# Hybrid attention and HGRN2 block on one core: q and k stored by other rows, loaded in one transfer and earlier; scores ahead of transposes; the merge's sums in another order

## The chip, the core and the metric

The kernel runs on one core of a Trainium2 chip, as one program. TensorE (PE) multiplies, VectorE (DVE), ScalarE (ACT) and GpSimd (POOL) do the elementwise work, SyncE (SP) and GpSimd issue DMA transfers, which 16 DMA engines carry. The metric is the time of the program on the device in microseconds; less is better.

## The reference

One encoder layer on x of 1024 tokens x 1024 channels, all in float32. From `h = rms_norm(x)` one input projection makes everything else:

```python
z = jnp.einsum('bsd,dc->bsc', h, w_in[layer].astype(f32))
qkv_a, g_a, q_b, zf_fwd, zf_bwd, i_b, g_b, zgate_a, zgate_b = jnp.split(z, split_points, axis=-1)
```

Branch A is dilated window attention: three groups of 8 heads of 64 channels, dilation 1, 4 and 16, 64 keys to each side. q and k are normed per head; scores get a bias by relative distance, then a softmax. The three groups' outputs are merged per head by their softmax denominators and multiplied by `silu(g_a)`. Branch B is a gated linear recurrence, forward and backward, over 8 heads of 128 channels. Each branch is projected to 1024 channels:

```python
merged = jax.nn.sigmoid(zgate_a) * y_a + jax.nn.sigmoid(zgate_b) * y_b
h_res = h_res + jnp.einsum('bsd,de->bse', merged, w_out[layer].astype(f32))
```

## The kernel before, in words

**Products.** A float32 product is made of three float32r products: each operand is split into a high part and a low part (hi x hi, hi x lo, lo x hi). Weights come in pages of 128 x 512 from DRAM; ScalarE makes the high part `whi` (a copy), and VectorE, GpSimd or an accumulating DMA the low part `wlo` (the page less `whi`); `Builder.low` names which. A ring of nine split pages stands between that work and TensorE.

**Stages.** In order of time: the norm of x and the values of attention (to 142 us in the profile); the *block stage*, in which most of the input projection is done in 27 blocks, each of which forms a 2 x 2 block product with seven products instead of eight (`run_quads`, to about 668 us); *attention*, mixed with further wide products (to about 845); the *merge* of the three groups, under wide products too (to about 933); the recurrence of branch B (to about 1220); and the two output projections, again by seven products.

**The order of the work.** The program is written by a planner, while it is built. `Plan` keeps a modelled time for each engine. Tasks wait in a list with a priority and are emitted by `tick` as soon as their inputs are ready by the model, lowest priority number first; small products of TensorE (scores, transposes, values) wait in another list, and `burst` emits those that are ready between wide products, in the order of their kind. Each engine then runs its own list strictly in that order, and semaphores hold an instruction until what it needs is there. So an instruction that waits holds all that stands behind it on its engine.

**The block stage.** SP loads the raw pages as pairs, `qraw`, into a ring of three. For each of the seven products of a block ScalarE splits a page; VectorE forms differences of pages for four of them. Results of the q and k blocks are normed (squares on ScalarE, sums by a product `nss`, a Newton step on VectorE), and `scaled` writes them, in the order of residues modulo the dilation, into a ring of four tiles `ny`; its task `out` stores a tile of 128 x 512 to `qkD` in DRAM, in pieces of 2 KB, 512 or 128 bytes per row by the dilation. There are 48 such stores, 16 for each group; half of those of group 2 are in pieces of 2 KB. A tile of `ny` is written again only when its store is done with it.

**Attention.** `attention_start` ends the block stage's pools, opens those of attention, and adds its loads: four pages of h that were set aside (`back_load`), then for each group and half of the heads k, q, the bias, and eight tiles of values. `load_heads` brings a megabyte of q or k in four transfers of 32 partitions each, since the rows of a head pair lie in `qkD` by channel. `scores` (kind 3) writes to PSUM `sc`; VectorE adds the bias and finds the maximum, ScalarE takes the exponentials; `turn` and `turn_pairs` (kind 1) transpose them (`pT`); `pv` (kind 2) multiplies by the values (`o`). Small products of 64 x 64 or 64 x 128 tiles share TensorE's array; the transposes use it whole.

**Merge.** `spread_al` spreads the weights of the three groups by a product (`al`), and six operations of VectorE multiply, sum and gate.

Of the kernel before, what the change touches and what calls it, by code (L numbers as in the profile page):

```python
# [9 lines left out]
F32R = mybir.dt.float32r  # L10
# [3 lines left out]
OP = mybir.AluOpType  # L14
# [4 lines left out]
S = 1024  # L19
# [15 lines left out]
VR, PT = 10, 8  # L35
# [200 lines left out]
class Builder:  # L236
# [56 lines left out]
    def burst(self, merge, most=None):  # L293

        k = 0
        for t in sorted(self.small, key=lambda t: (t.kind, t.seq)):
            if t not in self.small or (t.prio and not merge):
                continue
            if max(self.when(t) + self.SLACK, self.bank.when(t.banks)) > self.p.t["pe"]:
                continue  # L300
            if self.bank.room(t.banks) and (t.room is None or t.room()):
                self.small.remove(t)
                t.fn()
                k += 1
                if most is not None and k >= most:
                    break
        return k
# [348 lines left out]
def hybrid_block(ctx, tc, a, out):  # L656
# [641 lines left out]

    att = {}

    def attention_start(now=False):
        if att or not (now or (not b.small and b.quiet())):
            return
        b.drain()
        gctx.close()
        sctx.close()
        p = hctx.enter_context(tc.tile_pool(name="h10b", bufs=1, side="right"))
# [3 lines left out]
        for n, k, shape in (("v", VR, [128, 256]), ("q", 2, [128, 2, S]), ("k", 2, [128, 2, S]),  # L1311
                            ("s", 6, [128, 3, 4, 64]), ("pt", PT, [128, 2, 2, 128]), ("os", 2, [128, 2, 2, 128]),
                            ("bias", 2, [128, 4, 256])):
            att[n] = b.ring(ap, "a" + n, k, shape)
        for e in range(2):
            hq[e][1, 0] = p.tile([128, 4, 512], F32R, name=f"hb{'hl'[e]}")
        for c in range(4):
            b.task("sp", [], lambda c=c: back_load(c), 1, stage.soon)
        for o, g in enumerate((2, 1, 0)):
            for hv in range(2):  # L1320
                soon = lambda n, k=2 * o + hv: att[n].soon() and (k == 0 or b.wire(3.5))
                for n, f in (("k", load_k), ("q", load_q), ("bias", load_bias)):
                    b.task("sp", [], lambda g=g, hv=hv, f=f: f(g, hv), 2, lambda n=n, soon=soon: soon(n))
                for i in range(8):
                    b.task("sp", [], lambda g=g, hv=hv, i=i: load_v(g, hv, i), 2, lambda soon=soon: soon("v"))

    def back_load(c):
        t = stage.get()
        s_.dma_start(t, h10D[c])
        b.task("act", [t], lambda: back_split(c, t), 2)  # L1330

    def back_split(c, back):
        hi, lo = hq[0][1, 0][:, c], hq[1][1, 0][:, c]
        a_.activation(hi, back, AF.Copy)
        v_.tensor_tensor(lo, back, hi.bitcast(F32), op=OP.subtract)
        stage.done(back)
        att["h"] = att.get("h", 0) + 1

    QT, KT, BIAS, V, left = {}, {}, {}, {}, {"in": 0, "out": 0, "turned": 0}

    def load_heads(t, at):
        for j in range(2):
            for col in range(2):
                s_.dma_start(t[64 * j + 32 * col:64 * j + 32 * col + 32],
                             at[col].rearrange("(p j c) t -> j c p t", p=2, j=2)[j])

    def load_k(g, hv):
        KT[g, hv] = att["k"].get()
        load_heads(KT[g, hv], qkD[g, hv, 2:4])
        score_tasks(g, hv)  # L1350

    def load_q(g, hv):
        QT[g, hv] = att["q"].get()
        load_heads(QT[g, hv], qkD[g, hv, 0:2])
        score_tasks(g, hv)

    def load_v(g, hv, i):
# [239 lines left out]
    def merge_maybe(now=False):  # L1597
# [140 lines left out]
    def evac_qe(h, u):  # L1738
# [4 lines left out]
            store(qD[h, u], t)  # L1743
        return f

    for pr in range(2):
        grs = [tok_group(pos, 128 * i, evac_early(pr, i), last=(i >= 6)) for i in range(8)]
        for k in range(7):
            if pr == 0 and k == 4:
                attention_start(True)  # L1750
                b.until(lambda: att.get("h", 0) == 4)
            b.run_unit(grs[k:k + 1] if k < 6 else grs[6:])
            attention_start()
            merge_maybe()
# [835 lines left out]
```

## Time and profile before

| | before |
|---|---|
| time, median of 3 runs (lowest to highest) | 1420.7 us (1419.35 to 1420.76) |
| the profiled execution | 1421.55 us |
| its span, from the first to the last instruction | 1419.8 us |
| mean granted TensorE clock | 0.997 |
| TensorE busy | 1404.7 us (99%) |
| VectorE, ScalarE, GpSimd busy | 932.6, 840.7, 356.6 us |
| moved by DMA | 230.29 MB, mean 162 GB/s |

Times in the profile are microseconds from the start of the span, mean durations of groups are nanoseconds. A matmul's end is modelled and overlaps the next one's start, so what counts of TensorE is the distance between starts: 0.23 us for a wide product of 512 columns. A row of the waits reads: who, who ended the wait, total us, times, longest. A row of the DMA issues reads: what is written and from what, the issuing queue, how often, KB each, and the median us from issue to landing, where the trace has all its marks. The chain of waits is followed back from the last instruction: start, length, what.

### The profile page before, as it was taken

Reading aid. Unit: us, or ns where it says so; the run is one execution under the profiler, and the core shown is the slowest. Engines: PE = TensorE matmul, PEld = TensorE weight load, DVE = VectorE, ACT = ScalarE, POOL = GpSimd, SP = SyncE. Lnnn points to the kernel's source line nnn. Section 1 sums busy time; section 2 is a strip of 40 time slices with the busy share of each in tenths; the row PEclk is TensorE's granted clock in tenths of the full one; section 3 lists DMA queues with packets and bytes.
Section 4 is the critical chain, followed back from the end, with each engine's and each line's share of the span. In section 5 each row is a group of like instructions: output and inputs, shape, how many; then the busy total and the mean of one; then the engine's idle time right before and its main releaser. Section 6 shows DMA issues by size and latency. Waiting matters only on the chain.

```text
span 1419.8 us, 23915 instructions
## 1 busy us (share of the span) xinstructions
PE 1404.7 (99%) x8506; PEld 1168.3 (82%) x8506; DVE 932.6 (66%) x1889; ACT 840.7 (59%) x1831; POOL 356.6 (25%) x379
## 2 busy tenths in 40 slices
PE   9999999999999999999899999999999999999998
PEld 8788888788888888888778888888888888888887
DVE  6673556776776776331356657887878786358973
ACT  7743554665655646444577553577778784558461
POOL 0101434545433443334032110122222221001011
PEclk9999999999999999999999999999999999999999
DMA  7846568667633344423999429554444452778665
GB/s 238 187 134 188 171 183 190 146 174 172 165 102 99 96 123 136 157 104 126 251 264 261 134 67 318 177 141 124 114 120 120 116 137 73 233 243 218 185 166 137
DMA packets 178915, 230.29 MB, mean 162 GB/s; under 512 B 42227, under 2 KB 102923, under 8 KB 178284
## 3 DMA queue, kind: packets, MB, share of 16 engines
q1 hardware_dynamic: 160988, 193.19, 44.8%
q0 software_dynamic: 16944, 35.40, 13.8%
q8 instruction: 67, 1.10, 0.3%
q14 instruction: 52, 0.43, 0.1%
q10 hardware_dynamic: 864, 0.19, 0.1%
HBM read 168.77 MB, written 81.43 MB: 176 GB/s over the span
## 4 chain that ended last, share of the span: by engine, by line
PE 82%; DVE 7%; DMA 4%; ACT 4%; issue 2%; SPq 0%; POOL 0%; DVEq 0%; ACTq 0%; POOLq 0%
PE gp L60 26%; PE qA L60 18%; PE qE L60 9%; PE sA L60 6%; PE sE L60 5%; PE qC L60 4%; PE u L60 3%; PE oB L60 3%; PE sc L60 2%; PE o L60 2%; DMA qraw<-in_w_in_dram 2%; PE pT L60 1%; DVE ny L60 1%; PE U L60 1%; DMA raw<-in_w_in_dram 1%
## 5 line engine op out<-in xcount | busy, mean ns | idle before, releaser
L60 POOL TENSOR_TENSOR wlo<-qraw,whi 128x512 fp32r<-128x512 f32 x135 | 187.6, 1396 | 375.0 <-ACT whi L60 374.5
L60 ACT ACTIVATE whi<-qraw 128x512 fp32r<-128x512 f32 x189 | 117.8, 626 | 113.8 <-DVE qraw L60 53.1
L60 PE MATMUL gp<-hh,whi 128*128 128x512 f32 x264 | 109.8, 416 | 0.0
L60 DVE TENSOR_TENSOR qraw<-qraw,qraw 128x512 f32<-128x512 f32 x81 | 83.5, 1032 | 34.3 <-DMA qraw<-in_w_in_dram 21.1
L60 PE MATMUL gp<-hh,wlo 128*128 128x512 f32 x264 | 103.8, 393 | 0.0
L60 PE MATMUL gp<-hl,whi 128*128 128x512 f32 x264 | 103.1, 391 | 0.0
L60 ACT ACTIVATE as<-as,neg 128x192 f32<-128x192 f32 (+1 forms) x192 | 77.7, 409 | 25.7 <-DVE neg L60 25.7
L60 PE MATMUL qA<-hh,whi 128*128 128x512 f32 x216 | 84.0, 389 | 0.0
L60 PE MATMUL qA<-hl,whi 128*128 128x512 f32 x216 | 84.0, 389 | 0.0
L60 PE MATMUL qA<-hh,wlo 128*128 128x512 f32 x216 | 84.0, 389 | 0.0
L60 PE MATMUL gp<-whi,hh 128*128 128x512 f32 x192 | 79.6, 414 | 1.0 <-ACT stage L60 1.0
L60 ACT ACTIVATE whi<-raw 128x512 fp32r<-128x512 f32 x92 | 57.3, 626 | 34.4 <-DMA raw<-in_w_in_dram 10.7
L60 POOL COPY mm<-Bc 128x8 f32<-128x8 f32 x64 | 32.6, 539 | 177.7 <-DVE Bc L60 177.7
L60 PE MATMUL gp<-wlo,hh 128*128 128x512 f32 x192 | 75.7, 394 | 0.4 <-DVE wlo L60 0.4
L60 PE MATMUL gp<-whi,hl 128*128 128x512 f32 x192 | 75.5, 393 | 0.0
L60 DVE TENSOR_TENSOR wlo<-qraw,whi 128x512 fp32r<-128x512 f32 x54 | 37.6, 696 | 52.4 <-ACT whi L60 51.4
L60 DVE CUSTOM_DVE_ANT_0 as<-sc,abias 128x192 f32<-128x192 f32 (+1 forms) x192 | 48.6, 308 | 21.6 <-PE sc L60 11.3
L60 POOL DMA_DIRECT2D wlo<-in_w_in_dram x36 | 31.1, 863 | 114.3 <-ACT wlo L60 97.7
L60 PEld LDWEIGHTS gp<-hh,wlo 128*128 128x128 f32 x264 | 49.5, 188 | 11.1
L60 PEld LDWEIGHTS gp<-hh,whi 128*128 128x128 f32 x264 | 49.8, 189 | 8.3
L60 PEld LDWEIGHTS gp<-hl,whi 128*128 128x128 f32 x264 | 49.9, 189 | 8.0
L60 ACT ACTIVATE stage<-gp 128x512 f32<-128x512 f32 x39 | 22.7, 589 | 54.5 <-PE gp L60 43.7
(317 smaller groups left out, 4146.2 us busy)
## 6 DMA issues: line engine op xcount, KB each, us to landing
raw<-in_w_in_dram SPq DMA_DIRECT2D x84, 256.0 KB, 3.6
qraw<-in_w_in_dram SPq DMA_DIRECT2D x60, 256.0 KB, 3.6
qraw<-in_w_in_dram SPq DMA_DIRECT2D x24, 512.0 KB, 4.3
qkD<-ny SPq DMA_DIRECT2D x48, 256.0 KB, 3.3
wlo<-in_w_in_dram POOLq DMA_DIRECT2D x36, 256.0 KB, 4.3
sg<-sgD SPq DMA_DIRECT2D x32, 256.0 KB, 2.9
eraw<-wsD SPq DMA_DIRECT2D x32, 256.0 KB, 3.0
sgD<-stage SPq DMA_DIRECT2D x26, 256.0 KB, 2.2
```

Source lines behind the costliest of these rows:

```text
L60: got = f(*args, **kw)
```

## The change

It does six things.

1. *Stores.* The rows of q and k get another order in `qkD`: the row of a channel is now at 64 i + 32 x + c instead of in its own block of 128, so that a store of 128 rows goes to four places of 32 consecutive rows each.
2. *Loads.* With that order q or k of four heads is one transfer of 128 partitions instead of four of 32 (`load_heads` is gone).
3. *Room.* The pools for q, k and transposed weights, and the place for the four pages of h, move to the right side and are opened by a new `attention_room`, called right behind the block stage; the loads of h and of the first k and q become tasks there, with priority 1.5, and `quiet` does not count them.
4. *Burst.* While `eager` (in attention) the transposes, kind 1, are sorted as 3.5, behind values (2) and scores (3).
5. *Low parts.* From the merge on, `low` is "pool" instead of "dve": GpSimd makes the low parts of the pages there.
6. *Sums.* `spread_al` writes the second product in place in PSUM and adds all to `near`; there are still six operations.

```diff
-        for t in sorted(self.small, key=lambda t: (t.kind, t.seq)):
+        for t in sorted(self.small, key=lambda t: (t.kind if t.kind != 1 or not self.eager else 3.5, t.seq)):
...
-        return all(t.fn in (self.split_next_page, self.feed) for t in self.tasks)
+        return all(t.prio == 1.5 or t.fn in (self.split_next_page, self.feed) for t in self.tasks)
...
-            to = qkD[g, hv, 2 * e + col]
+            to = qkD[g, hv].rearrange("a p t -> (a p) t")[256 * e:256 * e + 256].rearrange("(i x c) t -> i x c t", i=4, x=2)[:, col]
             if g == 2 and e == 1:
-                s_.dma_start(to[:, 512 * half:512 * half + 512], o)
+                s_.dma_start(to[:, :, 512 * half:512 * half + 512], o)
             else:
-                s_.dma_start(to.rearrange("p (r u) -> p r u", r=R)[:, :, n * half:n * half + n],
+                s_.dma_start(to.rearrange("i p (r u) -> i p r u", r=R)[:, :, :, n * half:n * half + n],
                              o.rearrange("p (r u) -> p r u", r=R))
...
+    def attention_room():
+        sctx.close()
+        p = hctx.enter_context(tc.tile_pool(name="h10b", bufs=1, side="right"))
+        ap = actx.enter_context(tc.tile_pool(name="attnR", bufs=1, side="right"))
+        for n, k, shape in (("q", 2, [128, 2, S]), ("k", 2, [128, 2, S]), ("pt", PT, [128, 2, 2, 128])):
+            early[n] = b.ring(ap, "a" + n, k, shape)
+        for e in range(2):
+            hq[e][1, 0] = p.tile([128, 4, 512], F32R, name=f"hb{'hl'[e]}")
+        for c in range(4):
+            b.task("sp", [], lambda c=c: back_load(c), 1.5, stage.soon)
+        for f in (load_k, load_q):
+            b.task("sp", [], lambda f=f: f(2, 0), 1.5)
...
-    def load_heads(t, at):
-        for j in range(2):
-            for col in range(2):
-                s_.dma_start(t[64 * j + 32 * col:64 * j + 32 * col + 32],
-                             at[col].rearrange("(p j c) t -> j c p t", p=2, j=2)[j])
...
-        KT[g, hv] = att["k"].get()
-        load_heads(KT[g, hv], qkD[g, hv, 2:4])
+        KT[g, hv] = early["k"].get()
+        s_.dma_start(KT[g, hv], qkD[g, hv, 2:4].rearrange("a p t -> p a t"))
...
-        b.low = "dve"
+        b.low = "pool"
...
-        v_.tensor_tensor(nat(acc, 1), nat(al[1], 1), per(1), op=OP.mult)
+        v_.tensor_tensor(nat(al[1], 1), nat(al[1], 1), per(1), op=OP.mult)
         v_.tensor_tensor(nat(far, 2), nat(al[2], 2), per(2), op=OP.mult)
+        v_.tensor_tensor(near, near, al[1], op=OP.add)
         v_.tensor_tensor(near, near, far, op=OP.add)
-        v_.tensor_tensor(acc, acc, near, op=OP.add)
-        v_.tensor_tensor(acc, acc, gate, op=OP.mult)
+        v_.tensor_tensor(acc, near, gate, op=OP.mult)
...
+    attention_room()
     for pr in range(2):
```

Three places show how the instructions move. First SP's queue in the last third of the block stage: stores of a q and k block from `ny` tiles to `qkD`, and the loads of the next block's pages behind them. The last numbers of a row are the counts of the transfer's destination, outermost first. Before, and then with the change:

```order
L60 DMA sgD<-stage_4386 128x512
L60 DMA sgD<-spare_4511 128x512
L60 DMA qkD<-ny_4497 128x512
L60 DMA qkD<-ny_4495 128x512
L60 DMA qkD<-ny_4571 2048x1x32
L60 DMA qraw_4636<-in_w_in_dram 128x512 x2
```

```order
L60 DMA sgD<-stage_4386 128x512
L60 DMA sgD<-spare_4511 128x512
L60 DMA qkD<-ny_4497 4x32x512
L60 DMA qkD<-ny_4495 4x32x512
L60 DMA qkD<-ny_4571 4x512x32
L60 DMA qraw_4636<-in_w_in_dram 128x512 x2
```

No row has moved here; the destinations have 4 as their outermost count, where 128 and 2048 stood. The same holds for all 48 stores, and up to the last product of the block stage TensorE's rows are the same.

Second SP's queue at the start of attention: `gaD` is the last store of the block stage, `stage<-h10D` the four pages of h, `ak` and `aq` k and q, `abias` the bias.

```order
L60 DMA gaD<-spare_5854 128x512
L60 DMA raw_5874<-in_w_in_dram 128x2x256
L60 DMA ibD<-stage_5888 128x512
L60 DMA stage_5905<-h10D 128x512
L60 DMA stage_5907<-h10D 128x512
L60 DMA ak_5909<-qkD 32x2x1024 x4
L60 DMA aq_5914<-qkD 32x2x1024 x4
L60 DMA abias_5919<-skewD 64x4x64 x2
```

```order
L60 DMA gaD<-spare_5854 128x512
L60 DMA stage_5877<-h10D 128x512
L60 DMA stage_5879<-h10D 128x512
L60 DMA stage_5881<-h10D 128x512
L60 DMA ak_5883<-qkD 128x2x1024
L60 DMA aq_5885<-qkD 128x2x1024
L60 DMA raw_5893<-in_w_in_dram 128x2x256
L60 DMA ibD<-stage_5911 128x512
L60 DMA stage_5924<-h10D 128x512
L60 DMA abias_5926<-skewD 64x4x64 x2
```

k and q are one row each and stand ahead of the next weight page and of the store of `ibD`, which needs a product behind the block stage; the bias stays behind them.

Third TensorE in attention, behind the second scores of group 2: `sc` are scores, `pT` transposes, `gp` wide products.

```order
L60 MATMUL sc_6193<-ak_5909,aq_5914 64x64
L60 MATMUL sc_6192<-ak_5909,aq_5914 64x64
L60 MATMUL gp_6162<-whi_5708,hbh 128x512
L60 MATMUL gp_6162<-wlo_5709,hbh 128x512
L60 MATMUL gp_6162<-whi_5708,hbl 128x512
L60 MATMUL pT_6233<-ident,as_6026 128x128 x2
L60 MATMUL pT_6233<-ident,as_6027 128x128 x2
L60 MATMUL gp_6162<-whi_5731,hbh 128x512
```

```order
L60 MATMUL sc_6192<-ak_5883,aq_5885 64x64
L60 MATMUL sc_6193<-ak_5883,aq_5885 64x64
L60 MATMUL pT_6220<-ident,as_6039 128x128 x2
L60 MATMUL pT_6220<-ident,as_6040 128x128 x2
L60 MATMUL gp_6139<-whi_5752,hbh 128x512
L60 MATMUL gp_6139<-wlo_5753,hbh 128x512
```

Transposes now follow the scores in one burst instead of standing between wide products.

More of the change, by code (lines that the diff above doesn't have):

```diff
@@ L1299, in hybrid_block @@
     att = {}
+    early = {}
+    def attention_room():
[10 more added lines that the diff above has]
+            b.task("sp", [], lambda f=f: f(2, 0), 1.5)
     def attention_start(now=False):
@@ L1305, in attention_start @@
         gctx.close()
-        sctx.close()
-        p = hctx.enter_context(tc.tile_pool(name="h10b", bufs=1, side="right"))
         psum(2)
@@ L1310, in attention_start @@
         ap = actx.enter_context(tc.tile_pool(name="attn", bufs=1))
-        for n, k, shape in (("v", VR, [128, 256]), ("q", 2, [128, 2, S]), ("k", 2, [128, 2, S]),
-                            ("s", 6, [128, 3, 4, 64]), ("pt", PT, [128, 2, 2, 128]), ("os", 2, [128, 2, 2, 128]),
+        att.update(early)
+        for n, k, shape in (("v", VR, [128, 256]), ("s", 6, [128, 3, 4, 64]), ("os", 2, [128, 2, 2, 128]),
                             ("bias", 2, [128, 4, 256])):
             att[n] = b.ring(ap, "a" + n, k, shape)
[L1315 to L1318, printed above, removed]
         for o, g in enumerate((2, 1, 0)):
@@ L1321, in attention_start @@
                 soon = lambda n, k=2 * o + hv: att[n].soon() and (k == 0 or b.wire(3.5))
-                for n, f in (("k", load_k), ("q", load_q), ("bias", load_bias)):
+                for n, f in (("k", load_k), ("q", load_q), ("bias", load_bias))[2 if o == hv == 0 else 0:]:
                     b.task("sp", [], lambda g=g, hv=hv, f=f: f(g, hv), 2, lambda n=n, soon=soon: soon(n))
@@ L1329, in back_load @@
         s_.dma_start(t, h10D[c])
-        b.task("act", [t], lambda: back_split(c, t), 2)
+        b.task("act", [t], lambda: back_split(c, t), 1.5)
     def back_split(c, back):
@@ L1336, in back_split @@
         stage.done(back)
-        att["h"] = att.get("h", 0) + 1
+        blk["h"] = blk.get("h", 0) + 1
     QT, KT, BIAS, V, left = {}, {}, {}, {}, {"in": 0, "out": 0, "turned": 0}
-    def load_heads(t, at):
-        for j in range(2):
-            for col in range(2):
-                s_.dma_start(t[64 * j + 32 * col:64 * j + 32 * col + 32],
-                             at[col].rearrange("(p j c) t -> j c p t", p=2, j=2)[j])
     def load_k(g, hv):
-        KT[g, hv] = att["k"].get()
-        load_heads(KT[g, hv], qkD[g, hv, 2:4])
+        KT[g, hv] = early["k"].get()
+        s_.dma_start(KT[g, hv], qkD[g, hv, 2:4].rearrange("a p t -> p a t"))
         score_tasks(g, hv)
     def load_q(g, hv):
-        QT[g, hv] = att["q"].get()
-        load_heads(QT[g, hv], qkD[g, hv, 0:2])
+        QT[g, hv] = early["q"].get()
+        s_.dma_start(QT[g, hv], qkD[g, hv, 0:2].rearrange("a p t -> p a t"))
         score_tasks(g, hv)
@@ L1750, in hybrid_block @@
                 attention_start(True)
-                b.until(lambda: att.get("h", 0) == 4)
+                b.until(lambda: blk.get("h", 0) == 4)
             b.run_unit(grs[k:k + 1] if k < 6 else grs[6:])
```

## The prediction

> **What bounds the kernel now.** I read the busy shares first, then the chain of waits by stage, then the waits of TensorE alone.
>
> ```profile
> PE 1404.7 (99%) x8506; PEld 1168.3 (82%) x8506; DVE 932.6 (66%) x1889; ACT 840.7 (59%) x1831; POOL 356.6 (25%) x379
> 142.00:300.00 158.00, 156.75 (x691) 129.13 (x690) 101.01 (x121) 93.17 (x164) 70.73 (x62) 1.00 0.66 172
> 300.00:450.00 150.00, 150.00 (x664) 124.20 (x663) 104.32 (x121) 87.10 (x152) 62.36 (x50) 1.00 0.55 145
> 450.00:550.00 100.00, 100.00 (x443) 82.81 (x442) 74.41 (x86) 59.63 (x104) 39.07 (x26) 1.00 0.41 108
> 550.00:660.00 110.00, 110.00 (x487) 91.09 (x486) 44.86 (x54) 49.57 (x84) 38.26 (x30) 1.00 0.38 126
> ```
>
> The first line is the page's, the others are the table by stretches (start:end, length, then busy us of TensorE, its weight loads, VectorE, ScalarE, GpSimd, granted clock, DMA share, GB/s). TensorE has no idle time to speak of: whatever is removed elsewhere is worth nothing unless TensorE waited for it, and whatever makes TensorE wait is paid in full. From 142 to 668 us run the 27 blocks of seven products (the block stage); it stands at 516.75 busy of 518. But the chain of waits in that stage is not TensorE's everywhere:
>
> ```profile
> 205.99 2.73 PE qA L60 x12
> ...
> 218.07 7.69 DMA qraw<-in_w_in_dram
> ...
> 231.47 4.97 DMA qkD<-ny
> ...
> 239.60 7.66 DMA qraw<-in_w_in_dram
> ...
> 260.78 6.44 DMA qraw<-in_w_in_dram
> ```
>
> For 85 us (208 to 293) it goes through loads of weights and one of the very stores that the change rewrites: there a transfer that lands later moves the end. Elsewhere in the stage it is TensorE alone. Its waits, in the block stage (first line) and from 655 to 860:
>
> ```profile
> PE qA L60 <- ACT spare L60: 0.8, 1, 0.8
> ```
>
> ```profile
> PE sc L60 <- DMA aq<-qkD: 3.8, 2, 2.2
> PE gp L60 <- ACT stage L60: 2.2, 2, 1.2
> PE o L60 <- issue: 0.5, 1, 0.5
> ```
>
> So two places can move: the start of attention, where there is something to gain, and the block stage, where there is something to lose.
>
> **The stores of q and k, 48 of 256 KB.** TensorE's program is the same to the last product of the block stage; there only the destinations of these stores differ, and their outermost count falls from 128, 512 or 2048 to 4. I ask how many of the 16 DMA engines then carry one. What the traces show of shape:
>
> ```profile
> q1 hardware_dynamic: 160988, 193.19, 44.8%
> ...
> qraw<-in_w_in_dram SPq DMA_DIRECT2D x60, 256.0 KB, 3.6
> ...
> qkD<-ny SPq DMA_DIRECT2D x48, 256.0 KB, 3.3
> ...
> sgD<-stage SPq DMA_DIRECT2D x26, 256.0 KB, 2.2
> ak<-qkD SPq DMA_DIRECT2D x24, 256.0 KB, 6.2
> aq<-qkD SPq DMA_DIRECT2D x24, 256.0 KB, 8.8
> ...
> og<-oD SPq DMA_DIRECT2D x12, 512.0 KB, 5.2
> ...
> oh<-in_c_onehot_dram SPq DMA_DIRECT2D x1, 148.5 KB
> ...
> tabD<-tbs SPq DMA_DIRECT2D x3, 12.0 KB
> ```
>
> No transfer of before has 4 outside, so the price is bounded. Below: it is spread as now, and costs nothing. Above: one engine for each outermost row, four in all. I take the upper end, because the nearest rows are narrow ones: loads of 256 KB into 32 partitions (ak, aq) take 6.2 and 8.8 us where 128 partitions take 3.6, and twice the bytes (og) only 5.2. The Trainium skill, "DMA: Bandwidth & Descriptors", section "Why a DMA increments its semaphore by 16 and not by 1", says that a transfer runs on the largest number of engines up to 16 that divides the outermost dimension of both sides; for 4 and 128 that is four. The trace does not contradict it: the transfers with 33 and 8 rows (oh, tabD) are among the few without a landing time in this table, which a completion counted otherwise would explain; by the page the sum below stands as it is, and by an even spread it would be 32 us less.
>
> The price: queue q1 kept 0.448 x 16 x 1419.8 = 10,180 engine-us busy for 193.19 MB, 19.0 KB per engine-us. A store of 262,144 bytes is 13.8 engine-us: 0.86 us on each of 16, 3.45 on each of four. Stores in small pieces cost more. The landings of qkD alone, in 308:452 (512-byte pieces) and in 455:482 (128-byte pieces, one landing), beside those of sgD in 140:660 (2 KB, minimum 2.0):
>
> ```profile
> DMA to landing us min/median/max: 2.6/2.6/4.3
> ```
>
> ```profile
> DMA to landing us min/median/max: 4.2/4.2/4.2
> ```
>
> ```profile
> DMA to landing us min/median/max: 2.0/2.2/4.6
> ```
>
> Of the differences 0.2 us is a longer issue (its own durations go from 319 to 603 ns). That leaves 0.4 and 2.0 us more per engine: 1.26 and 2.9 on 16, 5.0 and 11.4 on four; for the 128-byte pieces, one landing under load, I take 8, between 5.0 and 11.4. With 24, 16 and 8 stores of the three kinds the four engines get 83 + 80 + 64 = 227 us instead of about 57: 170 us more in 526, on a share of 0.52, so 0.85. They can carry it, but what queues behind a pair of stores comes late. Two places on SP's queue:
>
> ```profile
> 215.04 2.94 SPq L60 DMA_DIRECT2D qkD<-ny  x2
> 218.07 2.00 SPq L60 DMA_DIRECT2D qraw<-in_w_in_dram  x2
> ```
>
> ```profile
> 455.22 1.59 SPq L60 DMA_DIRECT2D qkD<-ny  x2
> 456.90 3.37 SPq L60 DMA_DIRECT2D qraw<-in_w_in_dram  x3
> ```
>
> A load uses all engines and is done when the last four are. Behind the pair of 215 us it is late by 2 x 3.45 less the 3.0 us since the first store, about 4; behind 512-byte pairs by 2 x 5.0 - 3 = 7; behind the pair of 455 us by 2 x 8 - 2 = 14. In SP's order such a pair stands right ahead of a block's first load 4, 3 and 3 times for the three kinds; the other pairs have time to drain. ScalarE and VectorE split the pages in program order, so a late page also holds the PSUM copies behind it, and TensorE waits for those. How much it can take: the load of 239.60 came after 7.66 us instead of 3.6, 4 late, and TensorE idled 0.8, so the reserve was 3 us there; between 208 and 293, where two of the four late loads of the first kind and the quoted store lie on the chain itself, there is none; and from 300 us on, with DMA shares of 0.55 and less, I give it 6. Sum: 3 x 4 + 2 x (4 - 3) = 14 for the first kind, 3 x (7 - 6) = 3, 3 x (14 - 6) = 24: 41 us; with the 128-byte pieces at 5.0 it is 14 + 3 + 3 x (8 - 6) = 23. I take the middle, **+32 us**. Bounds: 0 if spread; with a reserve of 3 everywhere 14 + 12 + 33 = 59, and three long waits that each bring the clock loss of the next paragraph, 3 x 3.4, so 69.
>
> **The start of attention.** The change loads q, k and the four pages of h ahead of the first bias and values, q and k in one transfer each instead of four narrow ones. At the old place TensorE waited 3.8 us for aq (quoted), and then ran slow:
>
> ```profile
> 685.00:700.00 15.00, 11.21 (x128) 9.19 (x128) 6.50 (x57) 6.74 (x33) 0.56 (x1) 0.77 1.01 258
> ```
>
> A clock of 0.77 over 15 us is 3.4 us of full clock lost; the part of it that fell in the wait costs nothing, 2.5 fell into work. The Trainium skill, "TensorE: Matmul & The Clock Gate", Part 1, has the clock halve after an idle window of about 3.4 us; the two waits here, 3.8 us together, agree with it.
>
> In SP's new order k, q and three pages of h stand right behind the block stage, ahead of the first ib store; the scores come 78 products of 0.23 us behind its last product (72 before), 18 us. At the 258 GB/s of this stretch the 2 MB and 0.75 MB take 11 us. So the wait goes, and the slow clock with it: gain 3.8 + 2.5 = **6.3**; if the bias, which now stands last, is late instead, half of it.
>
> **The burst's order.** What a change of kind costs TensorE (scores sc, wide products gp, transposes pT):
>
> ```profile
> 767.19 1.57 PE L60 MATMUL sc<-ak,aq 64*128 64x192 f32 x16
> 768.69 0.50 PE L60 MATMUL gp<-whi,hh 128*128 128x512 f32 x1
> 769.03 0.39 PE L60 MATMUL gp<-wlo,hh 128*128 128x512 f32 x1
> ...
> 769.49 0.60 PE L60 MATMUL pT<-ident,as 128*128 128x128 f32 x4
> 769.85 0.48 PE L60 MATMUL gp<-whi,hh 128*128 128x512 f32 x1
> 770.17 0.39 PE L60 MATMUL gp<-wlo,hh 128*128 128x512 f32 x1
> ```
>
> Starts 0.23 us apart are the plain pace. After scores the first product takes 0.34: 0.11 for leaving the small tiles. Around transposes (0.36 + 0.32 against 4 x 0.11 + 0.23) it is 0.01: free. By the two orders scores or values are followed by a wide product 33 times before and 11 now; 21 times now a transpose follows them, which never happened before. Its price lies between 0, if only wide products pay, and the same 0.11: the gain is between 22 x 0.11 = 2.4 and 0.1. I take half, **1.2**. The other waits of attention (2.2 + 0.5) hang on ScalarE's queue and stay.
>
> **Merge.** Sixteen low parts move from VectorE to GpSimd:
>
> ```profile
> 860.00:935.00 75.00, 75.00 (x341) 62.10 (x340) 65.06 (x106) 40.09 (x71) 9.49 (x17) 1.00 0.77 251
> ```
>
> ```profile
> L60 POOL TENSOR_TENSOR wlo<-qraw,whi 128x512 fp32r<-128x512 f32 x135 | 187.6, 1396 | 375.0 <-ACT whi L60 374.5
> L60 DVE TENSOR_TENSOR wlo<-qraw,whi 128x512 fp32r<-128x512 f32 x54 | 37.6, 696 | 52.4 <-ACT whi L60 51.4
> ```
>
> GpSimd gets 16 x 1.4 = 22 us in 75 where it works 9.5, VectorE loses 11; the six operations of the merge stay six. TensorE is busy 75.00 of 75: nothing. If GpSimd were late with a page, 0.7 us each, 11 at most.
>
> **Sum.** The profiled execution took 1421.55 us (span 1419.8, 1.75 around it): + 32 - 6.3 - 1.2 = 1446.1. Its run lies 0.85 above the median of 1420.7, so I predict **1445**.
>
> **Rivals.** *The stores are spread as before* (chance 0.21): then only the gains remain, 1420.7 - 7.5 = 1413, and 1410 if attention's other waits (2.7) go too. For it: the bytes, pieces and 128 source partitions are the same. Against it: the narrow rows above. It decides from the number of engines: at 16 nothing is late. *Four engines, but the pages' ring of nine swallows most of it* (0.05): nine pages are 9 x 2.72 = 24 us of products, so a loss of 5 to 10 is possible if the ring is full; with the gains, 1418 to 1423. Against it: the 0.8 us idle at a load only 4 us late. *Attention loses* (0.04): with transposes last, values come later, VectorE's and ScalarE's copies bunch, and waits like the quoted 1.2 us appear five times more; with even stores 1420.7 - 6.3 + 12 = 1426. Only under the first rival would this decide the sign, from a loss of 7.5.
>
> The forecast itself has 0.70, with a range of its own of 1428 to 1470. The whole range of 8 in 10 reaches into the first rival: 1411 to 1470. A measurement of this kernel tells 0.2%, 2.8 us, from no change; faster 0.21, same 0.05, slower 0.74.
>
> **What will show it.** Right: the block stage is longer by some 32 us, mostly past 450 us, with waits of qA, qE, qC for ScalarE and of whi for qraw; the row of qkD<-ny has no landing time or a longer one; DMA share there hardly changes; attention starts without the wait for aq. Wrong: a block stage of 526 us; or a wait of sc for abias in place of aq; or more time between the first scores and the last values than before.

## The result, and the profile after

The changed kernel takes **1491.2 us** (median; 1489.67 to 1491.8), the kernel before 1420.0 beside it: a ratio of 1.0501, 95% interval 1.0485 to 1.0517. The forecast was 1445, range 1411 to 1470: the sign is right, the size is not. The loss is 71 us and not 25.

The page's head and its row of the stores, after:

```profile
span 1489.2 us, 23884 instructions
PE 1427.4 (96%) x8506; PEld 1179.1 (79%) x8506; DVE 928.6 (62%) x1873; ACT 839.6 (56%) x1831; POOL 381.0 (26%) x395
q1 hardware_dynamic: 159836, 193.18, 42.0%
qkD<-ny SPq DMA_DIRECT2D x48, 256.0 KB
```

TensorE, at 99% before, is at 96%. The engines' total work on queue q1 has not grown: 0.420 x 1489.2 = 625 us of all 16, 636 before. The stores' row has lost its landing time, and so have the rows of all other transfers on SP's queue, so the landings are read from single marks further below.

Where the time went is read from the block stage's ends. The chain of waits at its first product and at the first product behind it, before:

```profile
142.52 2.72 PE qA L60 x12
...
669.34 1.16 PE gp L60 x6
```

and after:

```profile
142.30 2.72 PE qA L60 x12
...
739.82 17.68 PE gp L60 x78
```

526.8 us before, 597.5 after: 70.7 more, of 69.4 more in the whole span. All else together gave back 1.3. What the 70.7 are, the waits of TensorE in that stretch and the table by stretches show (qA is one of a block's products, nss the norm's sums, `stage` and `spare` copies out of PSUM; columns as in the prediction; the table has the whole stage before in one row, then after in five stretches and as a whole):

```profile
PE qA L60 <- DVE stage L60: 12.6, 2, 7.0
PE qA L60 <- ACT stage L60: 12.1, 5, 4.5
PE qA L60 <- ACT spare L60: 10.8, 5, 4.7
PE nss L60 <- ACT nhi L60: 6.7, 2, 3.4
PE nss L60 <- DVE ny L60: 2.5, 1, 2.5
PE nss L60 <- DVE nlo L60: 2.2, 3, 0.9
```

```profile
142.52:669.34 526.82, 525.58 (x2318) 434.53 (x2317) 326.15 (x382) 292.74 (x509) 214.81 (x170) 1.00 0.52 143
```

```profile
142.30:300.00 157.70, 147.44 (x627) 119.71 (x627) 89.01 (x106) 79.10 (x141) 62.09 (x53) 0.97 0.60 155
300.00:400.00 100.00, 86.86 (x356) 70.08 (x355) 60.87 (x67) 46.00 (x81) 41.63 (x37) 0.93 0.59 138
400.00:500.00 100.00, 90.97 (x384) 73.52 (x383) 60.54 (x73) 54.41 (x96) 31.99 (x24) 0.97 0.36 105
500.00:600.00 100.00, 89.61 (x374) 72.45 (x373) 60.22 (x67) 45.26 (x79) 32.46 (x21) 0.95 0.38 85
600.00:739.80 139.80, 135.54 (x583) 110.99 (x582) 55.80 (x71) 66.51 (x113) 49.96 (x37) 0.98 0.42 128
142.30:739.80 597.50, 550.42 (x2317) 446.74 (x2317) 326.43 (x382) 291.28 (x509) 218.14 (x170) 0.96 0.48 126
```

The waits sum to 46.9 us, against 1.2 before. By the first and the last row of the table TensorE's idle time grew from 526.82 - 525.58 = 1.2 to 597.50 - 550.42 = 47.1 us, and its busy time grew by 24.8 us for the same products: together (45.8 and 24.8 before rounding) they are the 70.7. The granted clock of the stage is 0.96 where it was 1.00. The trace has ten periods in it at a clock of 0.50, 47.8 us together, so 23.9 us of full clock; for 7.2 of the 47.8 us TensorE was idle anyway, which leaves 20.3 that fell into work. So about a third of the loss is not waiting but the slow clock behind the waits. And the loss lies in every stretch: TensorE's idle time is 10.3, 13.1, 9.0, 10.4 and 4.3 us in the five stretches.

Two ways lead from a store to TensorE. The waits of ScalarE in the same stretch, before and after:

```profile
ACT whi L60 <- DVE qraw L60: 48.9, 29, 4.1
...
ACT ny L60 <- DMA qkD<-ny: 3.0, 3, 2.4
```

```profile
ACT whi L60 <- DVE qraw L60: 122.3, 48, 9.9
ACT ny L60 <- DMA qkD<-ny: 34.3, 12, 5.6
```

The first row is the pages that come late, which the prediction had. Part of that lateness is already in the issue: on SP's queue the longest issue of a page's load took 2.4 us before and 5.9 after, that of a store 0.6 and 5.2; why is not shown. The second row is a tile of `ny` that can't be written again until its store has landed, which it had not. Both stand on the chain of waits of after, in the region 217 to 262 us:

```profile
221.70 10.36 DMA qraw<-in_w_in_dram
...
237.74 10.73 DMA qkD<-ny
...
251.60 7.71 DMA qraw<-in_w_in_dram
```

### The profile page after: what moved, and what is told of

It reads as the page before. It is cut to its first block, busy times and chain, and to the rows that moved or that the text cites. A ratio compares the mean times of both kernels' runs of the same rounds, so it can differ in the third digit from the quotient of the medians.

```text
span 1489.2 us, 23884 instructions
## 1 busy us (share of the span) xinstructions
PE 1427.4 (96%) x8506; PEld 1179.1 (79%) x8506; DVE 928.6 (62%) x1873; ACT 839.6 (56%) x1831; POOL 381.0 (26%) x395
## 4 chain that ended last, share of the span: by engine, by line
PE 65%; DMA 12%; DVE 11%; ACT 7%; issue 3%; SPq 1%; POOL 0%; DVEq 0%; ACTq 0%; POOLq 0%
PE gp L60 26%; PE qA L60 8%; PE sA L60 6%; DMA qraw<-in_w_in_dram 6%; DMA qkD<-ny 6%; PE sE L60 4%; DVE ny L60 4%; PE qE L60 3%; PE u L60 3%; PE oB L60 3%; PE sc L60 2%; DVE qraw L60 2%; PE qC L60 2%; PE pT L60 2%; PE o L60 2%
## 5 line engine op out<-in xcount | busy, mean ns | idle before, releaser
L60 POOL TENSOR_TENSOR wlo<-qraw,whi 128x512 fp32r<-128x512 f32 x135 | 191.3, 1427 | 442.4 <-ACT whi L60 427.5
L60 DVE TENSOR_TENSOR qraw<-qraw,qraw 128x512 f32<-128x512 f32 x81 | 79.4, 981 | 87.3 <-DMA qraw<-in_w_in_dram 77.4
L60 PE MATMUL qA<-hh,whi 128*128 128x512 f32 x216 | 87.1, 403 | 12.8 <-DVE stage L60 12.6
L60 PE MATMUL qA<-S2h,whi 128*128 128x512 f32 x108 | 47.5, 440 | 22.9 <-ACT stage L60 12.1
L60 POOL COPY mm<-Bc 128x8 f32<-128x8 f32 x64 | 32.6, 539 | 129.0 <-DVE Bc L60 124.5
L60 PEld LDWEIGHTS qA<-hh,whi 128*128 128x128 f32 x216 | 42.3, 196 | 23.6 <-DVE stage L60 13.9
L60 POOL TENSOR_TENSOR wlo<-raw,whi 128x512 fp32r<-128x512 f32 x33 | 43.0, 1310 | 59.9 <-ACT whi L60 55.6
```

The source lines that it names most:

```text
L60: got = f(*args, **kw)
```

## Experiments: is it the four places, and how does the price grow?

**Sixteen places and eight.** One number of the store's destination. The two expectations say that the channels get mixed; that was an error of mine: with 8 or 16 places a channel stays inside its head, and q and k are exchanged alike, so the same is computed.

```diff
-  .rearrange("(i x c) t -> i x c t", i=4, x=2)[:, col]
+  .rearrange("(i x c) t -> i x c t", i=16, x=2)[:, col]
```

(`i=8` in rows8.)

> The changed kernel with one number of the stores other: 128 rows go to sixteen places of 8 rows instead of four of 32. The pieces, the bytes, the number of transfers and the order on every engine are the same; the rows then lie in another order than the loads of attention read, so that q and k come with their channels mixed and the output is another, which costs no time. Theory (the four outermost places put a store on four DMA engines, and all of the loss is in the block stage): sixteen marks for each store, block stage about 527 us as before, and in all 1491 less 70, about 1420; if the gain of 7.5 us forecast for attention was there and only hidden by the disturbance, 1413. Rival (it is the split destination itself, its more scattered rows or its descriptor of one more dimension, that costs): still near 1490.

> As the run with sixteen places, but eight of 16 rows (the output is another for the same reason). Theory: eight marks for each store and half the lateness of each; if the loss follows the lateness in proportion, about 1455; if waits shorter than a reserve of about 3 us are swallowed, as the prediction had it, 1420 to 1435. Rival of the scattered rows: about 1490.

Measured: sixteen places 1421.0 us, ratio to before 0.9997 (0.9985 to 1.0008); eight places 1435.1, ratio 1.0098 (1.0072 to 1.0125). The block stage of the two:

```profile
142.86:670.80 527.94, 526.34 (x2318) 434.25 (x2317) 328.39 (x382) 292.05 (x509) 216.85 (x170) 1.00 0.54 142
```

```profile
142.30:685.70 543.40, 530.99 (x2318) 436.24 (x2317) 328.87 (x382) 291.82 (x509) 215.25 (x170) 0.99 0.52 138
```

The pieces, the number of transfers and the order of the engines are those of the changed kernel, so neither the scattered rows nor the descriptor's form costs anything: the number of engines does. The semaphore marks of single stores in the trace (us from the issue to each mark) say it directly:

```
 4 places, 492.91 us:  0.94 | 5.43 5.68 6.74 6.87
 8 places, 214.92 us:  1.05 | 3.93 4.01 4.13 4.28 4.45 4.59 4.60 5.02
16 places, 215.38 us:  3.21 3.23 3.31 3.41 3.62 3.65 3.66 3.72 3.75 3.76 3.77 3.80 3.81 3.83 3.84 3.94
```

Four, eight and sixteen landings, and with less than sixteen one early mark beside them. This is what the Trainium skill states in "DMA: Bandwidth & Descriptors", section "Why a DMA increments its semaphore by 16 and not by 1" (the largest number up to 16 that divides the outermost dimension of both sides; each of these engines counts its own landing, and the issuing queue writes the rest at once); the trace agrees, with 4, 8 and 16 landings and the one early mark. By these marks the last landing of the 48 stores comes after a median of 3.4 us before, 3.8 with sixteen places, 5.1 with eight and 8.0 with four. The price grows faster than that: 0, 14 and 70 us.

**Half of the stores spread, and the groups one by one.**

```diff
+            if hv == 1:
+                for i in range(4):
+                    d, s = to[i], o[32 * i:32 * i + 32]
...
+                        s_.dma_start(d.rearrange("p (r u) -> p r u", r=R)[:, :, n * half:n * half + n],
+                                     s.rearrange("p (r u) -> p r u", r=R))
```

and, for one group at a time (`g == 2` in narrow_g2):

```diff
-  .rearrange("(i x c) t -> i x c t", i=4, x=2)[:, col]
+  .rearrange("(i x c) t -> i x c t", i=4 if g == 1 else 16, x=2)[:, col]
```

> The changed kernel with the stores of one half of the heads (24 of 48) written as four transfers of 32 rows each, the same rows at the same places, so that each of them is spread again; the other 24 go to four places at once as before. Theory: each narrow store costs by itself, so half of the 70 us is left, about 1455. Rival (the four engines are merely overloaded, and it is the backlog from one pair to the next that costs): well over half goes, 1430 or less.

> The changed kernel with four places for the sixteen stores of group 1 (pieces of 512 bytes) alone, and sixteen places for the other 32 stores. The prediction's sum gave these sixteen stores 3 us (three pairs, each 7 late against a reserve of 6). Rival, after the runs with eight places and with half of the stores narrow: every narrow store costs about the same, 70 / 48 = 1.5 us, so about 23 us here, 1440 to 1448.

> Four places for the sixteen stores of group 2 alone (eight in pieces of 128 bytes, eight of 2 KB), sixteen places for the others. The prediction's sum has 24 us for the pieces of 128 bytes and a third of 14 for the others: 29, about 1450. By the run with group 1 alone (23.6 us for sixteen stores) every narrow store costs about 1.5 us whatever its pieces: 1445. If the three groups' losses add, group 0 would be left with 70 less both.

Measured: half spread 1465.4 us (ratio 1.0314, 1.0286 to 1.0341); group 1 alone 1444.6 (1.0167, 1.0135 to 1.0199); group 2 alone 1442.9 (1.0152, 1.0125 to 1.0178). Over the run with sixteen places group 1 costs 23.6 us and group 2 21.9, some 1.4 to 1.5 us for a narrow store in both, whatever its pieces (two executions each, so some 4 us to either side of the 23.6 and the 21.9). 70.2 less both leaves 24.7 for group 0, the same again, if the groups add; group 0 alone was not run. The sum of the prediction, 3 us for group 1 and 29 for group 2, does not hold: group 1 by far, group 2 by 7 us. Half spread lost 44, not 35; it also writes the other 24 stores in 96 transfers of 64 KB, and what those cost by themselves was not measured, so it settles nothing beside the others.

**Two parts.** 64 rows of each store to four places, 64 to sixteen:

```diff
+  for h, i in ((0, 4), (1, 16)):
+      to = rows[256 * e + 128 * h:256 * e + 128 * h + 128].rearrange("(i x c) t -> i x c t", i=i, x=2)[:, col]
+      part = o[64 * h:64 * h + 64]
```

> The changed kernel with each store in two transfers of 64 rows: one to four places of 16 rows, the other to sixteen places of 4. The channels stay inside their heads, so the output is the same. By the price of the prediction (13.8 engine-us for 256 KB) the four busiest engines then have 1.73 + 0.43 = 2.2 us for a store, against 3.45 with four places and 1.73 with eight. Theory (what counts is how long the busiest engine has with a store): a little over the run with eight places (1435), so 1436 to 1448. Rival (what counts is that a transfer is narrow at all): as with four places, 1480 to 1490.

Measured: 1439.5 us (ratio 1.0128, 1.0101 to 1.0154). So four engines are not a fault in themselves. Ordered by the time that the busiest engine has with a store, by the prediction's price of 13.8 engine-us: 0.86, 1.73, 2.2 and 3.45 us, the loss is 0, 14, 18 and 70 us.

## Experiments: by which way does a late store reach TensorE?

**One ring longer.** Room for it comes from `spare`, five tiles instead of seven, which has a run of its own as the control.

```diff
-QRAW, SPARE = 3, 7
+QRAW, SPARE = 3, 5
-        blk["y"] = b.ring(p, "ny", 4, [128, 512])
+        blk["y"] = b.ring(p, "ny", 6, [128, 512])
```

The first pair of lines is spare5, both are spare5_ny6, and spare5_q4 has `4, 5` in the first alone.

> A control for the next two: the changed kernel (four places) with the ring of PSUM copies, spare, at five tiles instead of seven, which frees room. Theory: the ring is not what ends the waits, so 1490 to 1500, some more at most.

> As the control, with the freed room given to the ring of ny, six tiles instead of four: a late store then holds the norm's tiles less. In the changed kernel 35.1 us of idle time ahead of instructions on ny were ended by the landing of a store (3.0 before). If the late ny is what TensorE waits for in the end, a third or more of the 70 us goes: under 1468. If the late pages behind the stores are (the prediction's only path), nothing goes: the control's time within 5 us.

> As the control, with the freed room given to the ring of raw pages, qraw, four pairs instead of three: loads are issued one pair earlier, so a late page is late by less. If late pages are what TensorE waits for, a third or more of the 70 us goes: under 1468. If late ny is, the control's time within 5 us. If both are needed, neither of the two gains much alone.

Measured: control 1494.8 us, six `ny` 1477.8, four pairs of pages 1473.1 (ratios 1.0520, 1.0401 and 1.0367, the intervals some 0.004 to each side for the first two and 0.003 for the third). Neither gains a third of the 74 us, and neither stays within 5 us of the control, so both ways count and neither is the only one. The waits of ScalarE, of the control, of six `ny` and of four pairs:

```profile
ACT whi L60 <- DVE qraw L60: 121.1, 43, 9.3
...
ACT ny L60 <- DMA qkD<-ny: 8.1, 5, 3.3
```

```profile
ACT whi L60 <- DVE qraw L60: 139.6, 52, 9.1
```

```profile
ACT ny L60 <- DMA qkD<-ny: 46.7, 17, 6.5
...
ACT whi L60 <- DVE qraw L60: 24.2, 19, 2.5
```

With six tiles the wait for `ny` is gone, and that for pages has grown from 121 us to 140; with four pairs that for pages falls to 24, and that for `ny` rises from 8 to 47. Each ring moves the wait to the other way. In the control itself the wait for `ny` is 8.1 us, where the changed kernel has 34.3, at about the same time: the size of one wait of ScalarE does not tell what it is worth.

**Both rings.** The room for the second comes from `nlo` and `nhi`, one tile each.

```diff
-QRAW, SPARE = 3, 7
+QRAW, SPARE = 4, 5
-        blk["lo"] = b.ring(p, "nlo", 2, [128, 512], F32R)
-        blk["hi"] = b.ring(p, "nhi", 2, [128, 512], F32R)
-        blk["y"] = b.ring(p, "ny", 4, [128, 512])
+        blk["lo"] = b.ring(p, "nlo", 1, [128, 512], F32R)
+        blk["hi"] = b.ring(p, "nhi", 1, [128, 512], F32R)
+        blk["y"] = b.ring(p, "ny", 6, [128, 512])
```

The run os3_rings has these lines too, on sixteen places and with three tiles of `aos` (the edit below).

> The changed kernel (four places) with both rings longer: six tiles of ny and four pairs of qraw; the room comes from spare at five tiles and from one tile each instead of two for the parts of the squares, nlo and nhi. Six tiles of ny alone came out at 1478, four pairs alone at 1473, against 1495 for the control. Theory (a narrow store holds up both what waits for its tile and what is loaded behind it, and each ring covers only one of the two): the two gains add at least, 17 + 22, so 1456 or less, and well less if either was capped by the other. Rival (both rings only buy the same few us of slack): 1470 to 1480. The shorter nlo and nhi can only make it slower.

> Sixteen places and three tiles of aos (1411.9 us), with both rings of the block stage longer as in the run both_rings (six ny, four pairs of qraw, five spare, one nlo and nhi). With four places the two rings together took the time from 1491 to 1425. Theory (they only cover the lateness of narrow stores, which sixteen places do not have): the block stage stays within 2 us of 527.9 and the time within 1409 to 1414. Rival (the longer rings are better in any case, and the 66 us say little of the narrow stores): 10 us or more less, under 1402.

Measured: with four places and both rings **1424.9 us** (ratio 1.0025, 1.0012 to 1.0038). Its block stage:

```profile
142.50:675.40 532.90, 526.63 (x2318) 434.18 (x2317) 308.59 (x382) 294.38 (x509) 214.40 (x170) 1.00 0.53 141
```

532.9 us, though its stores land no earlier than in the changed kernel (median 8.7 us). With sixteen places and three `aos` the same rings gave 1414.8 (ratio 0.9961, 0.9947 to 0.9974), 0.8 us over the expected range and not better than without them (1411.9, below). So the longer rings don't speed the stage up; they cover the lateness of the narrow stores, and the two ways together account for the loss: 66 of the 70 us are gone, against 17 and 22 for one ring each.

## Experiments: where the gain of attention went

With sixteen places the stores cost nothing, and the forecast for that case was 1413, from 7.5 us of gains. It came out at 1421.0.

**Rows and loads of before; rows and loads alone.**

undo_rows is the changed kernel with parts 1 and 2 of the change taken back:

```diff
-            to = qkD[g, hv].rearrange("a p t -> (a p) t")[256 * e:256 * e + 256].rearrange("(i x c) t -> i x c t", i=4, x=2)[:, col]
+            to = qkD[g, hv, 2 * e + col]
...
-        s_.dma_start(KT[g, hv], qkD[g, hv, 2:4].rearrange("a p t -> p a t"))
+        load_heads(KT[g, hv], qkD[g, hv, 2:4])
```

r16_only is the other way round: these lines' reverse in the kernel before, with `i=16`, and nothing else of the change.

> The changed kernel with the stores and loads of the kernel before (one block of 128 rows for each store; q and k in four transfers of 32 partitions each); room, early loads, burst and merge stay. Theory: the block stage is back at 527 us and the time within 0.3% of the run with sixteen places, so about 1420, or 1413 if attention's gain was hidden; the narrow loads at the start of attention cost up to the 3.8 us for which TensorE waited for aq before, if the early place does not cover them.

> The kernel before with nothing but the stores to sixteen places and the loads of q and k in one transfer each; no earlier room, no other burst order, no other merge. With sixteen places the channels stay inside their head and are exchanged alike in q and k, so the scores and the output are the same. Theory (the loads of attention were late because each came in four narrow transfers): the wait of sc for aq falls from 3.8 us to under 2, and the time is 1 to 4 us under before. Rival (the loads are late because they are issued late, whatever their form): the wait stays near 3.8 and the time is that of before.

Measured: rows and loads of before inside the changed kernel 1423.8 us (ratio 1.0015, 0.9999 to 1.0032); sixteen places and whole loads inside the kernel before **1416.1** (ratio 0.9966, 0.9954 to 0.9978). The wait for aq is gone in both, but only the kernel with whole loads gained time: with narrow loads at the early place other waits came (0.6 to 2.9 us, for aos, av and as). The two differ in more than the loads, since undo_rows has the new order of the burst too, which costs 4 us below; beside the run with sixteen places, which has that order and whole loads, undo_rows is 2.8 us slower. From the first score to the first `kT` of the recurrence (the tile view's first and last start us) the kernel before, undo_rows and r16_only take, in this order, 928.9 - 687.9 = 241.0, 246.6 and 237.3 us (the profiled execution of undo_rows, 1426.3 us, was its slowest of ten):

```profile
L60 PE MATMUL sc<-ak,aq x624: 218/311/427, 687.9 to 832.8; 64*64 64x64 f32 x92, 64*128 64x192 f32 x60, 64*128 64x128 f32 x4
L60 PE MATMUL kT<-ident,sk x112: 270/272/273, 928.9 to 1188.3; 128*128 128x128 f32 x112
```

```profile
L60 PE MATMUL sc<-ak,aq x624: 218/267/684, 685.5 to 835.5; 64*64 64x64 f32 x92, 64*128 64x192 f32 x60, 64*128 64x128 f32 x4
L60 PE MATMUL kT<-ident,sk x112: 270/272/273, 932.1 to 1191.4; 128*128 128x128 f32 x112
```

```profile
L60 PE MATMUL sc<-ak,aq x624: 218/218/428, 685.9 to 827.3; 64*64 64x64 f32 x92, 64*128 64x192 f32 x60, 64*128 64x128 f32 x4
L60 PE MATMUL kT<-ident,sk x112: 270/272/273, 923.2 to 1182.6; 128*128 128x128 f32 x112
```

**Burst and merge of before, and a third tile of aos.** In the run with sixteen places the wait for aq is gone. Two others stand in the same stretch, of which the second was there before (2.2 us) and the first was not; the chain of waits ahead of the first goes through a store of attention's output:

```profile
PE pT L60 <- ACT aos L60: 3.7, 1, 3.7
PE gp L60 <- ACT stage L60: 2.8, 2, 1.7
```

```profile
708.44 8.12 DMA oD<-aos
```

```diff
-  (t.kind if t.kind != 1 or not self.eager else 3.5, t.seq)
+  (t.kind, t.seq)
...
-        b.low = "pool"
+        b.low = "dve"
...
-  ("os", 2, [128, 2, 2, 128])
+  ("os", 3, [128, 2, 2, 128])
```

The first pair of lines is burst0, the second, with the sums of before, merge0, the third os3, and the first and third os3_burst0.

> The changed kernel with sixteen places for the stores (the run of that name, 1421.0 against 1421.7 before) and the burst's old order, transposes first. The prediction gave the new order 1.2 us (bounds 0.1 to 2.4): then this run is 1.2 us slower than the run with sixteen places. Rival (the new order makes the wait of pT for aos, 3.7 us in that run, which the kernel before has not): that wait goes, and this run is 1 to 4 us faster, 1417 to 1420.

> The changed kernel with sixteen places and the merge of before: low parts on VectorE from there, and the sums in the old order. The prediction put the merge at nothing: then the stretch from the first alT to the first kT, 68.9 us in the run with sixteen places and 70.3 before, and the total, stay within a microsecond. Rival: VectorE holds TensorE there, and this run is 1 to 2 us slower.

> The changed kernel with sixteen places and three tiles instead of two for the outputs of attention (aos, stored to oD by GpSimd's queue). In the run with sixteen places the chain of waits from 708 to 717 us goes through one such store of 8.1 us, behind which VectorE writes the next aos, and TensorE waits 3.7 us for it and then runs at half clock for 3.4. Theory (attention's forecast gain of 6 us was taken by this wait): it goes, with the slow clock, and the time is 3.7 + 1.7 = 5 us lower, 1415 to 1417. Rival (the store is late because the transfers ahead of it are many, and the tiles are only where it shows): another wait comes in its place, and the time stays at 1420 to 1422.

> Sixteen places, three tiles of aos, and the burst's old order. Each of the two alone against the run with sixteen places: 9 us less (three tiles) and 4 us less (old order). If the old order gained by moving the wait for aos, which three tiles take away, the two do not add: 1411 to 1413. If it gained elsewhere, 1407 to 1410.

All four on sixteen places. Old burst order 1417.0 us (ratio 0.9969, 0.9960 to 0.9978); old merge 1420.0 (0.9989, 0.9979 to 0.9999); three tiles **1411.9** (0.9941, 0.9928 to 0.9953), 9 us less where 5 were expected; three tiles and old order 1413.0 (0.9945, 0.9927 to 0.9963). The waits of TensorE from 660 to 880 us with three tiles, the one line that is left:

```profile
PE gp L60 <- ACT stage L60: 1.2, 1, 1.2
```

The merge is worth nothing that can be told. The new order of the burst costs 4 us as long as `aos` has two tiles and nothing with three, so what it costs hangs on that ring and not on the passage from small to wide products; with three tiles the 1.1 us between the two orders cannot be told from nothing. That the order alone makes this wait is not shown: r16_only has the old order and the same wait (3.3 us), and still is faster. With three tiles the kernel is 0.6% faster than before, and better than both kernels; what three tiles are worth in the kernel before, or beside whole loads alone, was not run.

## Why the prediction was right or wrong, point by point

- **The bound, and that the stores go to four engines: right.** TensorE's waits were paid in full; four marks; total DMA work unchanged; waits of qA for ScalarE and of whi for qraw, as foretold. With sixteen places nothing is lost, as the first rival had it for even stores.
- **"They can carry it, but what queues behind a pair of stores comes late": half of the way.** The engines did carry it (with both rings longer the stage takes 532.9 us with the same narrow stores), and pages did come late. But the sum followed only that way. A late store also keeps its tile of `ny`, a ring of four, and the norm's next step waits for that (34.3 us of ScalarE, 3.0 before). Only with both rings longer did the loss go.
- **The lateness of 4, 7 and 14 us by pieces, for 10 pairs, against a reserve of 0 to 6 us: the term that failed.** Its 32 us (41 and 23 at its ends, 59 with a reserve of 3) measured 70.7: 45.8 of idle time and 24.8 of longer busy time, most of it the slow clock. The price hangs on no kind of piece: groups 0, 1 and 2 cost about 25 (by difference), 24 and 22 us, where the sum of 41 had 9, 3 and 29. The reserve of 6 us from 300 us on was not there: TensorE idled 32.6 us between 300 and 600, as well before 450 us as behind, where the prediction had looked for "mostly past 450 us". And the latenesses were mis-sized by piece too: with no reserve at all they give 11, 21 and 47 us for the three groups, too little for pieces of 2 KB and too much for those of 128 bytes. That only the ten pairs ahead of a block's first load cost anything was not tested by itself. The upper bound of 69 us comes close to the 70.7 by luck: it is 59 of waits and 10 of clock.
- **The clock: left out of the middle value.** It was in the upper bound alone, as three long waits of 3.4 us each; it measured 20 to 25. Had the sum been right on the waits, it would still have missed a third. Nor do the two waits of the kernel before agree with an idle window of 3.4 us, as the prediction has it: the half clock starts at 688.30 us, when only the first of the two, 2.2 us long, had passed.
- **Start of attention, -6.3: the wait went, the gain did not come.** No wait for aq is left. But the next one, for `aos`, stands behind it with a slow clock of its own (0.50 from 717.38 to 720.79 us in the run with sixteen places), and TensorE's waits from 660 to 880 us sum to 6.5 us there as they did before. The prediction did ask what would be late next, and named the bias; it was a store. And the whole loads alone take the wait for aq away and gain 4.6 us; the early place adds nothing that shows (1417.0 us with it and the old order of the burst). The 1413 forecast for even stores is reached only with a third tile of `aos`, which the prediction does not have.
- **Burst, -1.2: wrong sign here**, 4 us lost with two tiles of `aos`, none with three.
- **Merge, 0: right**, within what can be told.
- **Rivals.** "Attention loses" was priced at 12 us; with sixteen places one new wait of 3.7 us came, with 1.7 of slow clock, enough to eat most of the gain. That the ring of nine pages swallows most of the loss is refuted by the 70.7 us.

## What to carry to other kernels

Look at the outermost count of both sides of every transfer: here 16 instead of 4, by a permutation of rows that is as good as the other, is worth 70 us. When a transfer gets slower, follow two things and not one: what is queued behind it, and what its own tile holds up until it lands; only both rings together covered it, and a test of one alone gave back a quarter. And count with each wait of a few microseconds the slow clock that can follow it.

## What was unexpected of the hardware

The clock falls to half behind short waits, and for whole units of time. Three stretches of the changed kernel (columns as above; the clock is the seventh entry): 2.73 us between two starts, the half clock after it, and a stretch with a wait of 0.8 that brought none:

```profile
350.43:353.16 2.73, 0.39 (x2) 0.00 (x0) 2.04 (x3) 2.12 (x4) 0.46 (x1) 1.00 0.04 14
...
354.14:357.55 3.41, 3.41 (x9) 2.69 (x9) 2.78 (x4) 2.19 (x4) 2.87 (x4) 0.50 0.38 57
470.00:478.00 8.00, 7.20 (x32) 5.61 (x31) 0.78 (x2) 3.80 (x8) 2.58 (x2) 1.00 0.22 62
```

The ten such periods of the block stage last 3.41 or 6.83 us, and their starts (234.67, 248.33, 309.77, 354.14, 367.79, ... 610.14 us) lie whole multiples of 3.413 us apart, as on a fixed grid. By that, a wait is dear or free by where it falls, and with eight places it was so: 1.8 us of waiting at 294 us brought half clock, 2.5 us at 376, which lie astride a mark of the grid, did not. Cutting all 19 traces of this case into units on that grid gives a bound: after a unit at full clock in which TensorE idled 1.95 us or more, the next was at half clock, in 60 of 60; under 1.68 us it never was (108 units with more than 0.6 us idle); between, it went both ways. So about half a unit of idle time is enough. The Trainium skill, "TensorE: Matmul & The Clock Gate", Part 1, names an idle window of about 3.4 us that is free-running; the length of the periods and their grid agree, but no wait need fill it.
